# The pooled layer's input of one sequence moved out of its out-projection into the other sequence's pooled layer

## Chip, cores and metric

The kernel runs on one core of a Trainium2 chip. The metric is the device time of one execution in microseconds, as the median of several executions. TensorE is PE in all views (PEld its weight loads), VectorE is DVE, ScalarE ACT, GpSimd POOL, SyncE SP.

## What is computed

Two sequences of 1024 tokens and width 1024, the prompt (s = 0) and the sample (s = 1), go through two layers with shared weights. Layer 0 is attention with an out-projection, layer 1 a pooled layer. Cut to what matters here:

```python
def _pool_mixer(h, w_in, w_grp, scale, w_out):
    u, gate = jnp.split(h @ w_in, 2, axis=-1)
    pooled = win_sum / cnt - u32.reshape(b, s, POOL_GROUPS, POOL_GROUP_DIM)
    mixed = jnp.einsum('bsgc,gcd->bsgd', pooled.astype(h.dtype), w_grp)
    mixed = mixed * scale.reshape(POOL_GROUPS, POOL_GROUP_DIM)
    y = mixed.reshape(b, s, POOL_WIDTH) * jax.nn.silu(gate)
    return y @ w_out

for l in range(DEPTH):
    shift, scl, gate = jnp.split(mod[:, None, :], 3, axis=-1)
    h = _rmsnorm(x, pre_norm[l]) * (1.0 + scl) + shift
    m = _attn_mixer(h, ...) if l % 2 == 0 else _pool_mixer(h, ...)
    x = x + gate * _rmsnorm(m, post_norm[l])
```

All is float32. The kernel gets float32 products from pairs: each operand is split into a rounded part (hi) and the rest (lo), and three matmuls make one product. So every operand of a matmul needs a copy (hi) and a subtraction (lo).

## The kernel before

The order of the program is: layer 0 of the prompt (until about 816 us), its out-projection (`outproj0(0)`, to 943), the KV projection of the sample (to about 1003) and its attention, its out-projection (`outproj0(1)`, from about 1645 to 1760), the pooled layer of the sample (`layer1(1)`, to about 2052), the pooled layer of the prompt (`layer1(0)`). A scheduler orders the instructions of each engine from the program's order and its own costs; each engine then runs its list in order. Nearly all DMAs are issued by SP, in order. A DMA's completion goes to one of eight lanes, and a DMA waits for the one issued eight before it on its lane.

**Out-projection** (`outproj0`, L1039). Eight tiles of 128 tokens. For tile i PE makes y times w_out, 48 matmuls of 128x512 into a PSUM slot S of two (`out_mm`, L986 to L991); tiles 0 to 3 have their y split beforehand (yw), tiles 0 and 1 are mostly computed before the attention ends (`out_pre`). For tiles 4 to 7 y is loaded and split one tile ahead in `load_ys` (L1052; `load_y`, L978). Then, per tile: Square on ACT with the sum of squares (L1101), jk = S times pg on DVE (L1102), which frees the slot, the reciprocal root on POOL (L124, L126), xt = jk r + xt on DVE (L1104), and the DMA of xt to x1_d (L1105, in the views x_d). The xt and x1_d of a tile are of the form "(t m r) d -> t r m d": tile t holds 128 tokens in the permuted order that the attention uses. After that the input of the pooled layer is made: `normed` (L246: Square L249, for the prompt a product L252, for the sample product and addition L254, L255, on POOL except in the last two tiles) and, one tile later, eight transposes with `perm` (`turned`, L257, L263). For the prompt the result goes to DRAM (`put_stash`, L278: copies L284 and L282, DMA hs_d L285), for the sample to the split hT in SBUF (`put_hT`, L269). `run_h` takes a step of these transposes at every second k of a tile.

In `outproj0(0)` two other things run beside it: the first weights of the next stage (`prefetch`, eight ws of 128 KB, splits L329 and L330) and the layer-0 input of the sample: `h_affine` (L300) loads eight xk of 512 KB in tiles of the yh buffers and makes hT by hi (ACT, L319), product and sum (DVE, L320) and lo (L321, half on DVE, half on POOL).

**Pooled layer** (`layer1`, L1117). Four groups g of 256 channels. For each: u by two `lin` of 48 matmuls into S slots (three now), the windows on POOL and DVE (`pool_ct`), two gates (`lin` and `gate_ct`), the mixed product (`mixed`, L1202 ff.; yf L1206, y L1209, L1210), and after the u of group g the output product of group g - 1 (`outp`, 8 tiles of 12 matmuls, L1228 to L1230, added into m by DVE, L1252). The pooled layer of the prompt starts with `h_affine` from hs_d (L1126), before its first `lin` (`lin_c`, L1133 to L1135).

```python
            x_ = nc.tensor.transpose(T[:, k * P : (k + 1) * P], x[:, kk * P : (kk + 1) * P], idm)
...
            self.normed(op, xt[i], hx, jk, g1, sh1, nc.vector if i >= NT - 2 else None)
            put = self.put_stash(op, i, self.hs_d) if s == 0 else self.put_hT(hN, i)
            late = [self.turned(hx, perm, put)]
```

Of the kernel before, what the change touches and what calls it, by code (L numbers as in the profile page):

```python
# [13 lines left out]
P = 128  # L14
# [45 lines left out]
class Trunk:  # L60
# [196 lines left out]
    def turned(self, x, idm, put):  # L257
        nc = self.nc
        for b in range(2):
            T = self.ptile("T")  # L260
# [28 lines left out]
    def x_ahead(self, ap):  # L289
        nc = self.nc  # L290
        xv = self.t["xs"].rearrange("(hf p r) d -> r hf p d", hf=2, r=4)
        for i in range(NT):
            x = ap.tile([P, D], F32, name=self.n("xa"), tag="vb", bufs=2)
            nc.sync.dma_start(x, xv[i // 2, i % 2])
            yield
            xe = ap.tile([P, 2, 4, P], F32, name=self.n("xe"), tag="vb", bufs=2)
            self.normed(ap, x, x, xe.rearrange("p b k c -> p (b k c)"))
            yield
            yield from self.turned(x, self.ident, self.put_stash(ap, i, self.xn_d, one=xe))

    def h_affine(self, pool, hT, src, col, tags, bufs, ahead):
# [3 lines left out]
        def load():  # L305
            k = len(xk)
            if k < KT:
                xk.append(pool.tile([P, S], F32, name=self.n("xk"), tag=tags[k % len(tags)], bufs=bufs))
# [5 lines left out]
        for k in range(KT):  # L314
# [6 lines left out]
            (nc.gpsimd if k % 2 else nc.vector).tensor_tensor(lo, x, hi.bitcast(F32), ALU.subtract)  # L321
# [290 lines left out]
    def layer0(self, s, hT, ap, side, after_proj, open2, run_h, first=None):  # L612
# [67 lines left out]
        ahead = self.x_ahead(ap) if s == 0 else None  # L680
# [207 lines left out]
        def finish_A(h):  # L888
# [37 lines left out]
            nc.sync.dma_start(self.y_d[s, ch : ch + HD, :], z[HD:P])  # L926
# [112 lines left out]
    def outproj0(self, s, wo, op, hN, pre, prefetch):  # L1039
        nc, t = self.nc, self.t  # L1040
        xsrc = (t["xp"] if s == 0 else t["xs"]).rearrange("(t m r) d -> t r m d", m=32, r=4)
        x1o = self.x1_d[s].rearrange("(t m r) d -> t r m d", m=32, r=4)
        hq, late = [], []
        ys, xt = {}, {}
# [6 lines left out]
        def load_ys(i):  # L1051
            if 4 <= i < NT:  # L1052
                ys[i] = []
                for f in range(2):
                    y0 = op.tile([P, 4, P], F32, name=self.n("y0"), tag="y0", bufs=3 - s)
                    ys[i].append(op.tile([P, 2, 4, P], F32R, name=self.n("yh"), tag="yh", bufs=4))
                    self.load_y(s, i, y0, ys[i][f], 4 * f, 4 * f + 4, 0)
# [10 lines left out]
        perm = op.tile([P, P], F32, name=self.n("perm"), tag="perm")  # L1068
        pg = self.mrow(op, 0, s, 2, "pg")
        load(0)  # L1070
        load(1)
        nc.sync.dma_start(perm, t["k_perm"])
        hN_of = g1 = sh1 = None
# [6 lines left out]
        pf = prefetch(op)  # L1080
        for i in range(NT):
            if i >= 1:
                load(i + 2)
            if i >= 3:
                load_ys(i + 1)
            if i < 2:
                ps = pre[0][i]
            else:
                ps = self.ptile("S")
                for k in range(KT):  # L1090
                    yh, q = (pre[1][i], k) if i < 4 else (ys[i][k // 4], k % 4)
                    self.out_mm(ps, yh, q, wo, k, k == 0, k == KT - 1)
# [5 lines left out]
            hx = op.tile([P, D], F32, name=self.n("hx"), tag="hx", bufs=2)  # L1098
            ss = op.tile([P, 1], F32, name=self.n("ss"), tag="ss", bufs=6)
            jk = op.tile([P, D], F32, name=self.n("jk"), tag="jk", bufs=2)  # L1100
            nc.scalar.activation(hx, ps, AF.Square, accum_out=ss)  # L1101
            nc.vector.tensor_tensor(jk, ps, pg, ALU.mult)  # L1102
            r = self.rstd(op, ss, D, 1)
            nc.vector.scalar_tensor_tensor(xt[i], jk, r, xt[i], op0=ALU.mult, op1=ALU.add)  # L1104
# [7 lines left out]
        hq += late  # L1112
        for _ in pf:
            pass
        return run_h

    def layer1(self, s, hT, lp, hp, run_h, open_l2):  # L1117
# [4 lines left out]
        if s == 0:  # L1122
            hc = lp.tile([P, 2, KT], F32, name=self.n("hc"))
            nc.sync.dma_start(hc, self.mod_d[1, 0, 0:2].rearrange("c (k p) -> p c k", p=P))
            for _ in self.h_affine(lp, hT, self.hs_d, hc, ("sg1", "wa"), 2, 2):
                pass  # L1126
# [87 lines left out]
        def outp(parts, first, last, xs=None):  # L1214
            for i in range(NT):
                ps = self.ptile("S")
# [15 lines left out]
                if half:  # L1232
# [8 lines left out]
                    ss = lp.tile([P, 1], F32, name=self.n("ss"), tag="ss", bufs=4)  # L1241
# [11 lines left out]
                if last:  # L1253
                    ss = lp.tile([P, 1], F32, name=self.n("ss"), tag="ss", bufs=4)
# [21 lines left out]
        wu = wu0  # L1276
        for g in range(4):
            tail = s == 0 and g == 3
            wo = None
            if g and not tail:  # L1280
# [3 lines left out]
            for ct in range(2):  # L1284
                p = lp.tile([P, 2, S], F32R, name=self.n("pT"), tag="pT", bufs=2)
                pool_ct(g, pss[ct] if pss else lin(wu, ct), p)
                pT.append(p)
            if s == 1 and g == 0:
# [3 lines left out]
                self.psum("A", "SSS")  # L1292
            wgt = self.l1_block(wp, t["pwin"][2 * g + 1])
# [296 lines left out]
```

## Time and profile before

| what | value |
|---|---|
| median of 3 runs | 2353.71 us (2350.28 to 2356.88) |
| profiled execution, own time | 2351.0 us |
| its span, mean granted clock of TensorE | 2349.2 us, 0.964 |
| PE busy | 2140.3 us (91%) |
| DVE, ACT, POOL busy | 1562.4 (67%), 1065.3 (45%), 1009.8 us (43%) |
| DMA | 189.14 MB, 81 GB/s in the mean |

The busy shares are means over stages that differ. Where time could come from is read by stage: from the granted clock and the DMA share of a stretch, and from what PE waited for in it. The view of waits puts a wait down to the instruction or transfer that came last. A page's DMA digit is the busy share of the core's 16 DMA engines in tenths.

### The profile page before, as it was taken

Reading aid. Unit: us, or ns where it says so; the run is one execution under the profiler, and the core shown is the slowest. Engines: PE = TensorE matmul, PEld = TensorE weight load, DVE = VectorE, ACT = ScalarE, POOL = GpSimd, SP = SyncE. Lnnn points to the kernel's source line nnn. Section 1 sums busy time; section 2 is a strip of 40 time slices with the busy share of each in tenths; the row PEclk is TensorE's granted clock in tenths of the full one; section 3 lists DMA queues with packets and bytes.
Section 4 is the critical chain, followed back from the end, with each engine's and each line's share of the span. In section 5 each row is a group of like instructions: output and inputs, shape, how many; then the busy total and the mean of one; then the engine's idle time right before and its main releaser. Section 6 shows DMA issues by size and latency. Waiting matters only on the chain.

```text
span 2349.2 us, 38580 instructions
## 1 busy us (share of the span) xinstructions
PE 2140.3 (91%) x13777; PEld 1904.1 (81%) x13777; DVE 1562.4 (67%) x3463; ACT 1065.3 (45%) x2435; POOL 1009.8 (43%) x1445
## 2 busy tenths in 40 slices
PE   6998899999998776899999999987689999999998
PEld 3987788899998655898898999986468888778887
DVE  7788888776767653577778767776345455673536
ACT  6355555666666431256657666764221111320112
POOL 3776665123534332553321235343234345573552
PEclk9999999999999887999999999998899999999999
DMA  6123343111212353310011112122423111441113
GB/s 256 49 86 117 96 120 98 47 45 55 70 50 66 101 179 120 96 33 19 19 37 33 45 54 68 52 68 86 131 85 91 41 59 50 142 168 41 56 43 148
DMA packets 162641, 189.14 MB, mean 81 GB/s; under 512 B 16200, under 2 KB 127920, under 8 KB 162448
## 3 DMA queue, kind: packets, MB, share of 16 engines
q1 hardware_dynamic: 162112, 186.21, 25.3%
q8 instruction: 109, 1.79, 0.3%
q14 instruction: 84, 0.69, 0.1%
q10 hardware_dynamic: 144, 0.26, 0.0%
q0 software_dynamic: 192, 0.20, 0.0%
HBM read 144.43 MB, written 42.18 MB: 79 GB/s over the span
## 4 chain that ended last, share of the span: by engine, by line
PE 41%; DVE 7%; DMA 4%; ACT 3%; issue 2%; POOL 2%; SPq 1%; POOLq 0%; DVEq 0%; ACTq 0%
PE S L1135 5%; PE S L1134 5%; PE S L1133 5%; PE J L394 3%; PE J L396 3%; PE J L395 3%; PE S L1228 2%; PE S L1229 2%; PE S L1230 2%; PE H L720 2%; PE T L758 1%; DVE E L738 1%; DVE mx L721 1%; PE O L771 1%; DMA x_d<-xt 1%
## 5 line engine op out<-in xcount | busy, mean ns | idle before, releaser
L330 POOL TENSOR_TENSOR w<-ws,w 128x256 fp32r<-128x256 f32 (+1 forms) x418 | 391.9, 950 | 377.4 <-DVE w L329 266.0
L394 PE MATMUL J<-w,hT 128*128 128x256 f32 x1664 | 481.3, 289 | 2.9 <-ACT xj L407 2.1
L396 PE MATMUL J<-w,hT 128*128 128x256 f32 x1664 | 476.9, 287 | 3.1 <-DVE hT L1354 2.8
L395 PE MATMUL J<-w,hT 128*128 128x256 f32 x1664 | 477.5, 287 | 0.9 <-POOL w L330 0.7
L329 DVE CAST w<-ws 128x256 fp32r<-128x256 f32 (+1 forms) x420 | 186.9, 468 | 214.4 <-PE S L1135 77.9
L394 PEld LDWEIGHTS J<-w,hT 128*128 128x128 f32 x1664 | 318.0, 191 | 7.2 <-ACT xj L407 3.9
L396 PEld LDWEIGHTS J<-w,hT 128*128 128x128 f32 x1664 | 317.9, 191 | 5.6 <-DVE hT L1354 3.4
L395 PEld LDWEIGHTS J<-w,hT 128*128 128x128 f32 x1664 | 318.0, 191 | 4.3 <-POOL w L330 2.6
L738 DVE TENSOR_TENSOR E<-T,E 128x512 fp32r<-128x512 f32 x384 | 262.0, 684 | 83.3 <-ACT E L737 81.0
L737 ACT ACTIVATE E<-T 128x512 fp32r<-128x512 f32 x384 | 226.3, 597 | 200.0 <-PE T L758 72.5
L727 ACT ACTIVATE P<-H,mx 128x512 f32<-128x512 f32 x256 | 173.7, 685 | 109.4 <-DVE mx L722 95.5
L1135 PE MATMUL S<-hT,w 128*128 128x512 f32 x512 | 199.8, 391 | 2.7 <-POOL w L330 2.7
L1134 PE MATMUL S<-hT,w 128*128 128x512 f32 x512 | 200.0, 391 | 1.7 <-DVE hT L321 1.7
L1133 PE MATMUL S<-hT,w 128*128 128x512 f32 x512 | 199.3, 390 | 0.2 <-ACT hT L273 0.2
L721 DVE TENSOR_REDUCE mx<-H 128x1 f32<-128x512 f32 x256 | 173.7, 682 | 33.5 <-PE H L720 31.6
L758 PE MATMUL T<-identr,P 128*128 128x128 f32 x1024 | 163.1, 274 | 3.7 <-DVE E L738 3.1
L771 PE MATMUL O<-E,v 128*128 128x256 f32 x512 | 144.1, 303 | 16.1 <-DVE E L738 15.5
L837 ACT ACTIVATE P<-H,nm 128x256 f32<-128x256 f32 x256 | 117.7, 473 | 79.0 <-DVE nm L831 78.6
L770 PE MATMUL O<-E,v 128*128 128x256 f32 x512 | 147.5, 297 | 5.3 <-DVE X L792 2.8
L758 PEld LDWEIGHTS T<-identr,P 128*128 128x128 f32 x1024 | 123.0, 141 | 19.6 <-DVE E L738 2.4
L480 POOL TENSOR_TENSOR hl<-xj,hl 128x256 fp32r<-128x256 f32 x64 | 48.2, 756 | 208.7 <-DVE hl L479 154.6
L771 PEld LDWEIGHTS O<-E,v 128*128 128x128 f32 x512 | 97.2, 190 | 29.0 <-DVE E L738 26.7
(270 smaller groups left out, 5201.3 us busy)
## 6 DMA issues: line engine op xcount, KB each, us to landing
ws<-win SPq DMA_DIRECT2D x192, 128.0 KB
ws<-ada_w SPq DMA_DIRECT2D x128, 128.0 KB
ws<-pwin SPq DMA_DIRECT2D x60, 256.0 KB
vb<-v_d SPq DMA_DIRECT2D x64, 144.0 KB
xt<-xp SPq DMA_DIRECT2D x16, 512.0 KB
ada<-ada_w SPq DMA_DIRECT2D x16, 512.0 KB
y_d<-X SPq DMA_DIRECT2D x32, 256.0 KB
v_d<-v SPq DMA_DIRECT2D x64, 128.0 KB
```

The lines of the kernel that those rows point to most:

```text
L330: (nc.vector if dve_lo else nc.gpsimd).tensor_tensor(lo, src, hi.bitcast(F32), ALU.subtract)
L394: nc.tensor.matmul(ps, hi, w[:, 0, k, :], start=(k == 0), stop=False)
L395: nc.tensor.matmul(ps, hi, w[:, 1, k, :], start=False, stop=False)
L396: nc.tensor.matmul(ps, lo, w[:, 0, k, :], start=False, stop=(k == KT - 1))
L721: nc.vector.tensor_reduce(mx[:, c : c + 1], ps[c], axis=AX, op=ALU.max, negate=True)
L737: nc.scalar.activation(ov[0], Tv, AF.Copy)
L738: nc.vector.tensor_tensor(ov[1], Tv, ov[0].bitcast(F32), ALU.subtract)
L758: nc.tensor.transpose(T[:, (2 * e + i) * P : (2 * e + i + 1) * P], Pt[(h, 2 * g + i)][:, (2 * kp + e) * P : (2 * kp + e + 1) * P], self.ident)
L771: nc.tensor.matmul(O, st["v"][:, kk, :], pairs(ex, 1, e), start=False, stop=(kk == 7))
L1133: nc.tensor.matmul(ps[:, cs], w[:, 0, k, ws], hT[:, k, 0, cs], start=(k == 0), stop=False)
L1134: nc.tensor.matmul(ps[:, cs], w[:, 0, k, ws], hT[:, k, 1, cs], start=False, stop=False)
L1135: nc.tensor.matmul(ps[:, cs], w[:, 1, k, ws], hT[:, k, 0, cs], start=False, stop=(k == KT - 1))
```

## The change

- **The pooled layer's input of the prompt.** `outproj0(0)` ends a tile with the DMA to x1_d; second norm, transposes and hs_d are gone from it, and so is `perm`. `layer1(1)` has them instead: `x_ahead`, until now used in the attention, takes a source, a target and tags; for each of eight tiles it loads 128 rows of x1_d (plain order of tokens, one buffer xa), does `normed`, transposes into an S slot (`wide`) and writes hs_d. `more(n)` takes steps of it between u, outputs and gates of groups 0 to 3.
- **The affine step of the prompt** (`h_affine` from hs_d) moves from the start of `layer1(0)` into group 3 of `layer1(1)`: there the output product of group 2 comes behind the gates (`swap`), and each of its tiles is preceded by one step of `h_affine`. wo and the first weights of the next layer are loaded behind it.
- **Out-projections.** y of tile i + 2 is loaded at tile i (`load_y`) and split at k = 3 of the tile before (`split_y`); `prefetch` becomes `late_block` (four ws of 256 KB in the y0 buffers, from tile 6); xt has four buffers for the prompt; `h_affine` has two xk buffers of its own, starts at tile 1, and has its lo on POOL for odd k. For the sample the addition of `normed` is always on DVE. The order in which buffers are made differs.
- **The last y_d** of each attention is issued by ACT's queue.
- ss has six buffers in `layer1`.

```diff
-    def x_ahead(self, ap):
+    def x_ahead(self, ap, src, dst, tags, bufs, wide=False):
...
+            for _ in self.turned(x, self.ident, self.put_stash(ap, i, dst, one=xe), wide):
+                if not wide:
+                    yield
+            if wide:
+                yield
...
+    def late_block(self, wp, src):
+        nc = self.nc
+        self.wi += 1
+        w = (self.base if self.wi % 2 else wp).tile([P, 2, KT, 256], F32R, name=self.n("w"), tag="w", bufs=1)
+        ws = [wp.tile([P, 2, 256], F32, name=self.n("ws"), tag="y0", bufs=4) for _ in range(4)]
+        for q in range(4):
+            nc.sync.dma_start(ws[q], src[:, 2 * q : 2 * q + 2, :])
+        yield w
+        for q in range(4):
+            ks = slice(2 * q, 2 * q + 2)
+            self.split(w[:, 0, ks], w[:, 1, ks], ws[q])
             yield
...
-            nc.sync.dma_start(self.y_d[s, ch : ch + HD, :], z[HD:P])
+            (nc.scalar if h == heads[-1] else nc.sync).dma_start(self.y_d[s, ch : ch + HD, :], z[HD:P])
...
-                xt[i] = op.tile([P, D], F32, name=self.n("xt"), tag="xt", bufs=3)
+                xt[i] = op.tile([P, D], F32, name=self.n("xt"), tag="xt", bufs=4 - s)
...
+        def split_y(i):
+            if 4 <= i < NT:
+                if i > 4:
+                    new_y(i)
+                for y, z in zip(yh[i], y0[i]):
+                    nc.scalar.activation(y[:, 0], z, AF.Copy)
+                    nc.vector.tensor_tensor(y[:, 1], z, y[:, 0].bitcast(F32), ALU.subtract)
...
-            hN_of = self.h_affine(op, hN, self.xn_d, self.col[:, 1], ("yh",), 4, 3)
-            next(hN_of)
+            hN_of = self.h_affine(op, (("xk", 2),), 1, hN, self.xn_d, self.col[:, 1], (1, 3, 5, 7))
...
             if i >= 1:
                 load(i + 2)
-            if i >= 3:
-                load_ys(i + 1)
+            if i >= 2:
+                load_y(i + 2)
+            if i == 1 and hN_of:
+                next(hN_of)
...
-                        if i >= 4:
-                            next(pf, None)
+                    if k == 3:
+                        split_y(i + 1)
+                        if i == 6:
+                            pf = self.late_block(op, t["pwin"][0] if s else t["win"][8])
+                            self.kvw = next(pf)
...
-            self.normed(op, xt[i], hx, jk, g1, sh1, nc.vector if i >= NT - 2 else None)
-            put = self.put_stash(op, i, self.hs_d) if s == 0 else self.put_hT(hN, i)
-            late = [self.turned(hx, perm, put)]
-            if hN_of:
+            if s:
+                self.normed(op, xt[i], hx, jk[i], g1, sh1, nc.vector)
+                late = [self.turned(hx, perm, self.put_hT(hN, i))]
+            if hN_of and i >= 2:
...
+        if s == 1:
+            ahead = self.x_ahead(lp, lambda i: self.x1_d[0, i * P : (i + 1) * P, :], self.hs_d, ("xa", "yf"), 1, True)
...
+            if swap:
+                more(99)
+                hc = lp.tile([P, 2, KT], F32, name=self.n("hc"))
+                nc.sync.dma_start(hc, self.mod_d[1, 0, 0:2].rearrange("c (k p) -> p c k", p=P))
+                hNext = Halves(self, hp)
+                h_of = self.h_affine(lp, (("wa", 2), ("u", 2), ("wa", 2), ("u", 2), ("xa", 1)), 2, hNext, self.hs_d, hc, (1, 3, 5, 7))
+                next(h_of)
+                outp(prev, False, False, each=lambda i: next(h_of))
+                prev = []
```

**What moves on the engines.** Lines after the change have its own numbers; x_d is x1_d, y the buffers y0.

SP at the start of the prompt's out-projection. Before:

```order
L926 DMA y_d<-X_10884 64x1024
L243 DMA row_10922<-mod_d 128x1024
L1049 DMA xt_10924<-xp 128x1x1024
L1049 DMA xt_10926<-xp 128x1x1024
L1072 DMA perm_10921<-k_perm 128x128
L309 DMA xk_10929<-xn_d 128x1024
L309 DMA xk_10931<-xn_d 128x1024
L309 DMA xk_10933<-xn_d 128x1024
L1049 DMA xt_10935<-xp 128x1x1024
L309 DMA xk_10955<-xn_d 128x1024
L981 DMA y_1798_11090<-y_d 128x4x128
L981 DMA y_1800_11095<-y_d 128x4x128
```

With the change:

```order
L243 DMA row_10921<-mod_d 128x1024
L1072 DMA xt_10924<-xp 128x1x1024
L1072 DMA xt_10926<-xp 128x1x1024
L1072 DMA xt_10928<-xp 128x1x1024
L1072 DMA xt_10941<-xp 128x1x1024
L317 DMA xk_10943<-xn_d 128x1024
L1081 DMA y_1770_10957<-y_d 128x4x128
L1081 DMA y_1771_10958<-y_d 128x4x128
L317 DMA xk_11020<-xn_d 128x1024
L1081 DMA y_1780_11032<-y_d 128x4x128
L1081 DMA y_1781_11033<-y_d 128x4x128
L1147 DMA x_d<-xt_10924 4x32x1024
```

The last y_d has left SP's list, so row and the first xt stand behind loads of y alone. All four first xt come ahead of the first xk, and the loads of y for tiles 4 and 5 ahead of the first x_d; no hs_d stands between them.

DVE in the prompt's out-projection, about tile 4. Each jk frees a PSUM slot; xk and col belong to `h_affine`, ws and w to the weights of the next stage. Before:

```order
L983 TENSOR_TENSOR yh_11192<-y_1816_11191,yh_11192 128x512
L1102 TENSOR_TENSOR jk_11167<-S_11100,row_10922 128x1024
L320 TENSOR_SCALAR xk_11080<-xk_11080,col 128x1024
L1104 SCALAR_TENSOR_TENSOR xt_10965<-jk_11167,rr_11172,xt_10965 128x1024
L329 CAST w_11222<-ws_11247 128x256
L282 COPY hl_11244<-T_11239 128x512
L983 TENSOR_TENSOR yh_11197<-y_1818_11196,yh_11197 128x512
L983 TENSOR_TENSOR yh_11304<-y_1839_11303,yh_11304 128x512
L252 TENSOR_SCALAR hx_11165<-xt_10965,rr_11180 128x1024
L329 CAST w_11222<-ws_11263 128x256
L1102 TENSOR_TENSOR jk_11285<-S_11201,row_10922 128x1024
```

With the change:

```order
L328 TENSOR_SCALAR xk_11099<-xk_11099,col 128x1024
L1144 TENSOR_TENSOR jk_11089<-S_11036,row_10921 128x1024
L328 TENSOR_SCALAR xk_11104<-xk_11104,col 128x1024
L329 TENSOR_TENSOR hT_10917<-xk_11104,hT_10917 128x1024
L1146 SCALAR_TENSOR_TENSOR xt_10941<-jk_11089,rr_11095,xt_10941 128x1024
L1089 TENSOR_TENSOR yh_11221<-y_1790_11111,yh_11221 128x512
L328 TENSOR_SCALAR xk_11180<-xk_11180,col 128x1024
L328 TENSOR_SCALAR xk_11185<-xk_11185,col 128x1024
L329 TENSOR_TENSOR hT_10917<-xk_11185,hT_10917 128x1024
L350 CAST w_11300<-ws_11301 128x512
L1144 TENSOR_TENSOR jk_11170<-S_11115,row_10921 128x1024
```

The products of the second norm (L252) and the copies hl are gone. jk of tile 3 (jk_11089) stands behind the product of the fourth xk, and jk of tile 4 (jk_11170) behind the products of xk five to seven and the cast of the first ws. Seven rows later, with the casts of the other three ws ahead of it, follows the jk of tile 5.

DVE at the boundary of the pooled layers: m collects the output products, xk and hT belong to the affine step of the prompt. Before, with the last y of the sample and the last output product:

```order
L1210 TENSOR_TENSOR y_3580_23135<-yf_23133,y_3580_23135 128x1024
L1206 SCALAR_TENSOR_TENSOR yf_23151<-S_23138,sccol,sg_23100 128x1024
L320 TENSOR_SCALAR xk_23364<-xk_23364,hc_23362 128x1024
L321 TENSOR_TENSOR hT_23360<-xk_23364,hT_23360 128x1024
L320 TENSOR_SCALAR xk_23383<-xk_23383,hc_23362 128x1024
L1210 TENSOR_TENSOR y_3583_23153<-yf_23151,y_3583_23153 128x1024
L320 TENSOR_SCALAR xk_23393<-xk_23393,hc_23362 128x1024
L329 CAST w_23103<-ws_23116 128x512
L1252 TENSOR_TENSOR m_21615<-S_23156,m_21615 128x1024
```

With the change, the output product of group 2:

```order
L328 TENSOR_SCALAR xk_22936<-xk_22936,hc_22932 128x1024
L329 TENSOR_TENSOR hT_22934<-xk_22936,hT_22934 128x1024
L328 TENSOR_SCALAR xk_22938<-xk_22938,hc_22932 128x1024
L350 CAST w_23088<-ws_23089 128x512
L350 CAST w_23088<-ws_23093 128x512
L350 CAST w_23088<-ws_23097 128x512
L328 TENSOR_SCALAR xk_22959<-xk_22959,hc_22932 128x1024
L328 TENSOR_SCALAR xk_22940<-xk_22940,hc_22932 128x1024
L1291 TENSOR_TENSOR m_21389<-S_22945,m_21389 128x1024
L1228 SCALAR_TENSOR_TENSOR sg_22929<-sg_22929,S_22880 128x1024
L329 TENSOR_TENSOR hT_22934<-xk_22940,hT_22934 128x1024
```

The products of xk now stand among the additions of the output product of group 2, a gate and a mixed product earlier than before; the first of these additions (S_22945) is behind four of them and three casts.

## Rows read from the trace of the kernel before

**Rows 1.** The page, part 2: granted clock and DMA share in 40 slices.

```profile
PEclk9999999999999887999999999998899999999999
DMA  6123343111212353310011112122423111441113
```

**Rows 2.** Stages: length, busy time (instructions) by engine, clock, DMA share, GB/s.

```profile
821.80:943.00 121.20, 85.68 (x339) 68.02 (x339) 48.39 (x55) 32.44 (x50) 33.29 (x40) 0.85 0.49 150
943.00:1002.70 59.70, 53.09 (x441) 52.09 (x440) 34.33 (x79) 18.29 (x49) 31.98 (x50) 0.97 0.28 87
1651.20:1760.40 109.20, 84.95 (x337) 67.16 (x338) 45.94 (x49) 25.09 (x46) 30.70 (x40) 0.85 0.32 106
1760.40:2024.10 263.70, 263.45 (x1168) 217.51 (x1166) 130.17 (x135) 37.92 (x40) 115.43 (x95) 1.00 0.19 62
2024.10:2075.00 50.90, 41.62 (x168) 33.44 (x169) 48.29 (x36) 18.12 (x24) 41.31 (x29) 0.93 0.58 210
```

**Rows 3.** PE's waits, 816 to 1005 us: us in total, times, longest.

```profile
PE T L263 <- DVE hx L252: 21.4, 5, 6.9
PE S L989 <- ACT yh L982: 7.6, 1, 7.6
PE S L989 <- DVE jk L1102: 5.3, 2, 2.8
PE T L415 <- DVE hl L552: 3.9, 2, 3.5
PE T L263 <- DMA perm<-k_perm: 3.7, 1, 3.7
```

**Rows 4.** PE's waits, 1640 to 1765 us.

```profile
PE T L263 <- POOL hx L255: 22.2, 5, 8.4
PE S L989 <- DVE jk L1102: 8.3, 2, 6.2
```

**Rows 5.** PE's waits, 2015 to 2075 us.

```profile
PE S L1135 <- POOL w L330: 2.7, 1, 2.7
PE S L1134 <- DVE hT L321: 1.7, 1, 1.7
```

**Rows 6.** DMA share, GB/s in slices: 860 to 900; GB/s: 2020 to 2060.

```profile
DMA  3893922232222752225784559622773472562212
GB/s 112 195 364 139 303 102 102 111 102 102 111 98 102 234 172 102 111 102 181 249 249 128 137 154 286 210 99 102 249 200 114 150 258 102 187 210 78 78 57 95
...
GB/s 8 123 270 127 4 0 0 0 53 221 397 418 410 410 371 211 393 406 363 326 412 389 191 37 170 92 0 0 0 0 193 332 0 0 172 352 86 279 373 397
```

**Rows 7.** DMA issues, 816 to 945 us; SP's longest wait, 1640 to 1765.

```profile
hs_d<-hl SPq DMA_DIRECT2D x12, 256.0 KB
...
SPq L1049 <- DMA x_d<-xt: 29.1, 5, 9.5
```

**Rows 8.** PE's timeline (start, length); a chain row, 1690 to 1760 us.

```profile
1760.43 0.40 PE L1134 MATMUL S<-hT,w 128*128 128x512 f32 x1
...
1764.97 0.39 PE L1133 MATMUL S<-hT,w 128*128 128x512 f32 x1
...
1751.77 0.44 PE T L263 x4
```

**Rows 9.** PE's timeline, 940 to 980; a chain row, 816 to 1005 us.

```profile
955.19 0.66 PE L263 MATMUL T<-perm,hx 128*128 128x128 f32 x4 [2.46 <-DVE hx L252]
...
953.40 10.31 DMA hs_d<-hl
```

**Rows 10.** DVE's timeline, 1645 to 1672 us.

```profile
1649.94 1.23 DVE L1102 TENSOR_TENSOR jk<-S,row 128x1024 f32<-128x1024 f32 x1 [8.88 <-DMA row<-mod_d]
...
1664.22 1.28 DVE L254 SCALAR_TENSOR_TENSOR hx<-xt,rr,row 128x1024 f32<-128x1024 f32 x1 [5.89 <-DMA row<-mod_d]
```

**Rows 11.** Groups by line, shape, 1650 to 1760 us: busy, mean ns, idle.

```profile
L255 POOL TENSOR_TENSOR hx<-hx,row 128x1024 f32<-128x1024 f32 x6 | 14.5, 2420 | 12.4 <-DVE hx L254 6.2 <-DMA row<-mod_d 4.6 <-DMA y<-y_d 1.6
```

**Rows 12.** Groups by line, 2028 to 2075 us.

```profile
L320 DVE TENSOR_SCALAR xk<-xk,hc 128x1024 f32<-128x1024 f32 x6 | 8.8, 1473 | 1.1 <-ACT hT L319 1.1
```

More of the change, by code (lines that the diff above doesn't have):

```diff
@@ L307, in load @@
             if k < KT:
-                xk.append(pool.tile([P, S], F32, name=self.n("xk"), tag=tags[k % len(tags)], bufs=bufs))
+                tag, bufs = tags[k % len(tags)]
+                xk.append(pool.tile([P, S], F32, name=self.n("xk"), tag=tag, bufs=bufs))
                 nc.sync.dma_start(xk[k], src[k])
@@ L679, in layer0 @@
         rest = self.ada_rest(ap) if s == 0 else None
-        ahead = self.x_ahead(ap) if s == 0 else None
+        xv = self.t["xs"].rearrange("(hf p r) d -> r hf p d", hf=2, r=4)
+        ahead = s == 0 and self.x_ahead(ap, lambda i: xv[i // 2, i % 2], self.xn_d, ("vb", "vb"), 2)
         started = {0, 1, 2}
@@ L1121, in layer1 @@
         wu0 = kvw or self.l1_block(wp, t["pwin"][0])
[L1122 to L1126, printed above, removed]
         outap = t["yp"] if s == 0 else t["ys"]
@@ L1212, in mixed, with outp @@
             return yT
-        def outp(parts, first, last, xs=None):
+        def outp(parts, first, last, xs=None, each=None):
             for i in range(NT):
+                if each:
+                    each(i)
                 ps = self.ptile("S")
@@ L1253, in outp @@
                 if last:
-                    ss = lp.tile([P, 1], F32, name=self.n("ss"), tag="ss", bufs=4)
+                    ss = lp.tile([P, 1], F32, name=self.n("ss"), tag="ss", bufs=6)
                     if xs:
@@ L1276, in layer1, with more @@
         wu = wu0
+        ahead = hNext = h_of = None
+        if s == 1:
+            ahead = self.x_ahead(lp, lambda i: self.x1_d[0, i * P : (i + 1) * P, :], self.hs_d, ("xa", "yf"), 1, True)
+        def more(n):
+            for _ in range(n):
+                if ahead:
+                    next(ahead, None)
         for g in range(4):
             tail = s == 0 and g == 3
+            swap = s == 1 and g == 3
             wo = None
-            if g and not tail:
+            if g and not tail and not swap:
                 prev[0] = (prev[0][0], self.l1_block(wp, t["pwout"][g - 1]))
@@ L1287, in layer1 @@
                 pT.append(p)
+                if g:
+                    more(1)
             if s == 1 and g == 0:
@@ L1292, in layer1 @@
                 self.psum("A", "SSS")
+                more(2)
             wgt = self.l1_block(wp, t["pwin"][2 * g + 1])
@@ L1297, in layer1 @@
             self.split(wg[:, 0], wg[:, 1], ws)
-            if g and not tail:
-                outp(prev, g == 1, False)
+            if g and not tail and not swap:
+                outp(prev, g == 1, False, each=lambda i: more(i % 2))
                 prev = []
-            elif tail:
+            elif tail or swap:
                 prev[0] = (prev[0][0], self.l1_block(wp, t["pwout"][2]))
@@ L1304, in layer1 @@
                 wu = self.l1_block(wp, t["pwin"][2 * g + 2])
-            elif s == 1:
+            sgs = []
+            for ct in range(2):
+                sgs.append(gate_ct(lin(wgt, ct)))
+                more(1 if g else 2)
+            if swap:
[7 more added lines that the diff above has]
+                prev = []
+            if g == 3:
                 wo = self.l1_block(wp, t["pwout"][3])
-            sgs = [gate_ct(lin(wgt, ct)) for ct in range(2)]
-            if g == 3:
                 if s == 1:
                     self.kvw = self.l1_block(wp, t["pwin"][0])
-                else:
-                    wo = self.l1_block(wp, t["pwout"][3])
             ys = xs = None
@@ L1441, in run @@
             c_op, op = self.pool("op", R)
-            def prefetch(sp):
-                self.wi = 0
-                out = []
-                yield from self.block_gen(None, sp, t["pwin"][0] if s else t["win"][8], out=out, bufs=1 + s)
-                self.kvw = out[0]
-            run_h = self.outproj0(s, after.wo, op, hT, pre, prefetch)
+            run_h = self.outproj0(s, after.wo, op, hT, pre)
             st["c"].__exit__(None, None, None)
```

72 lines of the change are left out of this document (41 added, 31 removed).

## The prediction

> **What bounds the kernel now.** Start with the slices of the page: PE is nearly full except in two dips, around slices 14 to 16 and 28 to 29, and there the granted clock falls and the DMA digits rise to 5 and 4 [rows 1]. The table by stage gives these dips a name [rows 2]: the out-projection of the prompt (821.8 to 943.0, PE 85.7 busy of 121.2 us at clock 0.85) and that of the sample (1651.2 to 1760.4, 85.0 of 109.2, also 0.85). Between the second dip and 2024.1 PE has 263.5 of 263.7 us at clock 1.00: there every instruction added to PE adds its whole length. The list of PE's waits in each dip says what ends the idle time: in the first, the transposes T wait for hx (21.4 us, 2.5 of it behind the stretch) and for perm (3.7), the matmuls S for yh (7.6) and jk (5.3) [rows 3]; in the second, T waits for hx, made on POOL (22.2), and S for jk (8.3) [rows 4]. At the boundary of the two pooled layers PE waits 2.7 and 1.7 us in the first matmuls of the prompt's [rows 5].
>
> That is what the engines show. What stands behind hx and yh is the DMA digits. While xt is loaded or x_d written, they sit at 2 tenths for many slices together, with about 102 GB/s; in the pooled layer, where other transfers run, about 410 GB/s are reached [rows 6]. So a 512 KB xt or x_d takes 524 KB / 102 GB/s = 5.1 us on about a fifth of the engines, and another 512 KB transfer (xk, xa) 1.3 us on all. Each out-projection has eight xt and eight x_d. In the sample's, SP waited 29.1 us for earlier x_d before it could send the next xt, which is the same queue seen from the other end [rows 7].
>
> The Trainium skill has the reason (DMA: Bandwidth & Descriptors, "Why a DMA increments its semaphore by 16 and not by 1"): a transfer is spread over the largest number of engines up to 16 that divides the outermost dimensions of both sides, and takes the lowest-numbered ones. The write x_d has 4 there, and the trace agrees with its 2 tenths of 16 engines. It speaks against the change: these transfers keep their shape, so by it an out-projection can't come down to PE's own time; without it the sum below would be that of the first rival.
>
> **A. Out-projection of the prompt.** Removed: 48 of the 64 transposes and their waits, Square, product and copies of the second norm, and 12 of the 16 hs_d writes [rows 7]. The four xt buffers, y two tiles ahead and the split before its tile take away the waits for hx, perm and yh, (21.4 - 2.5) + 3.7 + 7.6 = 30.2 us. PE's own need: twenty matmuls go by in 1764.97 - 1760.43 = 4.54 us [rows 8], so a tile of 48 takes 10.9 us, six 65 us, and with the first jk wait and a few matmuls at the lower clock about 71 of 121. That would save 50. But tile 7 needs its slot, so jk of tile 5; this stands in DVE's order behind the cast of the fourth ws, which stands on SP behind x_d of tile 4. Before it come xt1 to xt7 and x_d0 to x_d4, 12 x 5.1 = 61 us; xk, 8 x 1.3 = 10; y and ws, 12 x 0.65 = 8. From 821.8 (xt1 waits for the last matmul of tile 1) that is 901 with no gap. I add 5 for issues that come late, since SP waits in order for DVE's xt and for earlier landings: 906; then 2 for cast and jk, 1 for yh, 12.5 for tile 7 (part at the low clock): 921.5 against 943.0. **A = -21.** Bounds: -50 (PE alone) and 0 (summed in this way, with 12 hs_d of 0.65 [rows 7], the old stretch has 8 us of transfers more and comes to 107 at most, and it took 121: if its other gaps come back, little is won). I take the value of the transfers, since the rows they come from are of this very stage.
>
> What is late next: jk3 stands behind the affine step of xk3, and this behind x_d0, x_d1, xt4 and xt5 in the DMA queues; so tiles 5, 6 and 7 should each wait for jk. Its own ACT queue for the last y_d wins nothing at the start: row comes earlier, xt1 doesn't.
>
> **B. KV projection (59.7 us).** The last transposes leave it, 16 at 0.44 us per four [rows 8], 1.8, with a wait of 2.5 for hx and the 3.9 for hl [rows 3, 9]; the latter came from DVE, held by an hs_d write of 10.3 [rows 9]. Together 8.2; late next are raw and ropB, which SP sends behind x_d of tile 6. **B = -5**, between 0 and -8.
>
> **C. Out-projection of the sample.** Nothing changes before about 1666: jk1 stands behind hx0, which needs the second row, landed at 1664.2 [rows 10]. The addition on DVE costs 1.2, like jk of the same size [rows 10], instead of 2.4 on POOL, six times [rows 11], on an engine busy 45.9 of 109.2 [rows 2]; POOL's 14.5 us go. From tile 3 PE alone needs 5 x 10.9 + 10 x 0.44 = 59, so the end would be 1726 (-34). By transfers: the third row and xt2 stand behind the second row, so they end about 1664.2 + 1.3 + 5.1 = 1671; then come 2 y, x_d0, x_d1, xt3 to xt6, x_d2 to x_d4, the other y and ws: 9 x 5.1 + 8 x 0.65 = 51, so 1722 to 1724; late issues 4, jk 2, tile 7 with four transposes 12: 1742. **C = -18**, between -34 and -6 (only the 8.4 of one wait for hx goes).
>
> **D. Pooled layer of the sample.** Added to PE: 64 transposes, 16 x 0.44 = +7.0, in a stage that has no idle time. Loads of 1.3 us and steps on DVE, ACT and POOL lie beside it: they are busy 130, 38 and 115 of 264 us [rows 2]. Removed at the boundary: 2.7 + 1.7 [rows 5], as hT of the prompt is made an output stage and a mixed stage earlier; the granted clock of 0.93 over those 51 us [rows 2] may give 1 back with the waits gone. New: the adds of output stage 2 now stand on DVE among the affine steps of xk, 8 x 1.5 [rows 12] and 4 x 1.2, and the first xk can't be read before the last hs_d is written. The stage has 8 tiles of 12 matmuls, 21.8 us by [rows 8], with 8 adds of the size of jk, 1.23 [rows 10]; so DVE has 26.6 us for 21.8, and I let PE wait for some of the excess, 3. +7.0 - 4.4 - 1 + 3 = **D = +4**, between -3 and +15.
>
> **Sum.** -21 - 5 - 18 + 4 = -40. The profiled execution took 2351.0 us (span 2349.2), the median of the runs 2353.7, which is 2.7 more; -40 from the median gives **2314 us**. A difference under 0.3%, 7 us, can't be told from none here.
>
> **Rivals.** *PE alone sets the out-projections*: the engines that xt leaves free take the rest, y and xk are never late, and A = -50, B = -8, C = -34, D = +4: 2266. For it: the waits of PE name DVE, ACT and POOL, not DMA [rows 3, 4]. Against: the flat 2 tenths [rows 6]. Something between the two, -45 to -75, is as likely as the full case.
>
> *Old gaps in new places*: DVE's strict order lets each late xk or ws hold jk, A = -8, C = -8, B = -3, D = +6: -13, 2341. For it: the old stretch took 14 us more than its transfers and last tile add up to.
>
> *Slower*: x_ahead has one xa and one xe buffer. Its transposes stand in PE's queue between the matmuls of the projections, so if a tile isn't ready, PE stops. A tile goes through the load, Square, rstd, the product, copies and the write of the one before; an hs_d write took 10.3 us beside other transfers [rows 9]. Each tile has more steps ahead of it than one lin of 10.9 us; but where loads of weights stand ahead, the wait could be 6 us for each of 8 tiles, +48, and with A + B + C = -44 the sum is +4 + 4: 2362. It decides from 5 us a tile on. For it: nowhere is PE as full as there, so there is nothing to hide it. Against: DMA is used at 0.19 there [rows 2], and transfers move at 400 GB/s.
>
> *It doesn't do what it says*: DVE and POOL set the slots of the output stage as before and the lower clock of each new gap takes the rest: within 7 us of before.
>
> **How the numbers follow.** The forecast (savings of 25 to 55) has 0.58, PE alone or half way to it 0.20, old gaps in new places 0.13, slower 0.06, no change 0.03. So faster 0.91, same 0.03, slower 0.06. The range for 8 in 10: its low end, 2272, is between the first rival half way (-65: 2289) and in full (2266), its high end, 2342, just above the second; what lies below and above holds about 0.08 and 0.10.
>
> **What would show it.** Right: waits T for hx gone from the prompt's out-projection, DMA digits at 2 tenths through most of it, waits of S for jk in front of tiles 5, 6 and 7, tile 7 ending 95 to 105 us after tile 1; about 91 us from tile 2 to 7 in the sample's; the pooled layer of the sample 5 to 10 us longer in PE, with no wait of transposes for xa over 1 us. Wrong: the out-projections at clock 1.00 without gaps (first rival), or single waits of 5 us on the S slots of the transposes (slower).

## The result and the profile after

The change made the kernel slower: 2369.65 us in the median (2367.53 to 2371.39) against 2352.89 (2350.28 to 2356.88) in the same session, a ratio of 1.0069 with a 95% interval of 1.0052 to 1.0087. The forecast was 40 us less; the result is 17 us more, outside the range.

The two profiled spans differ by 20.4 us (2369.6 and 2349.2). Cut at the same points of the program in PE's timeline, the difference lies here (us; the last two columns are runs of the section on the experiments):

| stage | before | after | after, split xt | before, split xt |
|---|---|---|---|---|
| start to the end of tile 1 of the prompt | 821.8 | 824.5 | 821.8 | 819.9 |
| prompt's out-projection, to the end of tile 7 | 121.2 | 115.4 | 73.9 | 75.5 |
| KV projection, to the first score matmul | 59.7 | 53.1 | 52.6 | 54.2 |
| attention, to the end of tile 1 of the sample | 642.3 | 643.0 | 643.2 | 644.6 |
| sample's out-projection, to the end of tile 7 | 115.4 | 122.6 | 80.9 | 79.9 |
| pooled layer of the sample | 292.1 | 318.5 | 309.3 | 293.1 |
| pooled layer of the prompt | 296.7 | 292.5 | 292.9 | 296.5 |

The prompt's out-projection won 6, the KV projection 7, the last layer 4; the sample's out-projection lost 7 and the sample's pooled layer 26. The time to the end of tile 1 lay between 819.7 and 824.5 us in all profiled runs of this study, so its 2.7 us are put down to no part of the change.

On the page the dips of the clock are slices 13 to 16 and 27 to 30, where before they were 14 to 16 and, counted in the same way, 29 and 30 [rows 1]. A slice is 59 us long, so 13 and 27 lie ahead of the out-projections; what the stages lost is read from the rows by stage below.

```profile
PEclk9999999999998878999999999988889999999999
DMA  6124333111212343200011121133323223341113
```

The stages, in the columns of [rows 2]:

```profile
824.50:939.90 115.40, 76.87 (x289) 61.15 (x290) 39.80 (x38) 20.45 (x30) 24.01 (x22) 0.81 0.42 125
939.90:993.00 53.10, 50.70 (x426) 49.45 (x425) 31.87 (x76) 16.21 (x45) 30.92 (x48) 1.00 0.24 81
1636.00:1758.60 122.60, 80.73 (x337) 64.25 (x338) 48.77 (x52) 25.38 (x48) 18.57 (x32) 0.83 0.33 103
1758.60:2077.10 318.50, 304.71 (x1330) 247.31 (x1329) 168.42 (x177) 67.13 (x84) 143.33 (x126) 0.97 0.32 97
```

The out-projections have a lower clock than before (0.81 and 0.83 after 0.85 and 0.85), and the pooled layer of the sample is no longer at 1.00. PE's waits in the first of them, where [rows 3] had four kinds (the fifth, for hl, stands behind the stage):

```profile
PE S L1011 <- DVE jk L1144: 38.6, 5, 15.1
```

One kind is left, but it is longer than all the old ones of that stage together: the 18.9 us for hx (21.4 without the 2.5 behind the stage), 3.7 for perm and 7.6 for yh went, jk grew from 5.3 to 38.6. In the sample's, against [rows 4]:

```profile
PE S L1011 <- DVE jk L1144: 24.1, 2, 19.0
PE T L267 <- DVE hx L255: 17.7, 3, 9.9
```

And in the pooled layer of the sample, where before there was no wait over 0.3 us until its end:

```profile
PE S L267 <- ACT xe L288: 6.7, 2, 5.5
PE S L1267 <- DVE m L1291: 2.7, 2, 2.5
PE S L1269 <- DVE y L1247: 1.9, 1, 1.9
PE S L267 <- DVE xa L252: 1.2, 1, 1.2
```

The last stage no longer has the waits of [rows 5], as forecast.

### The profile page after: what moved, and what is told of

It reads as the page before. It is cut to its first block, busy times and chain, and to the rows that moved or that the text cites. A ratio compares the mean times of both kernels' runs of the same rounds, so it can differ in the third digit from the quotient of the medians.

```text
span 2369.6 us, 38555 instructions
## 1 busy us (share of the span) xinstructions
PE 2147.6 (91%) x13777; PEld 1905.4 (80%) x13777; DVE 1558.7 (66%) x3461; ACT 1065.1 (45%) x2435; POOL 991.7 (42%) x1431
```

## The experiments

**Theory 1**: both out-projections are set by the xt loads and x1_d writes, which occupy few DMA engines; casts and affine steps in front of jk pass the lateness on to PE. The pooled layer lost by the transposes, their waits and the clock behind them. **Theory 2**: the order of DVE and SP costs the time whatever the transfers' shape, and the moved affine step costs the pooled layer.

**Split transfers, in the changed kernel and in the one before.** The same edit in both:

```diff
-                nc.sync.dma_start(xt[i], xsrc[i])
+                for q in range(4):
+                    nc.sync.dma_start(xt[i][32 * q : 32 * q + 32], xsrc[i][q])
...
-            nc.sync.dma_start(x1o[i], xt[i])
+            for q in range(4):
+                nc.sync.dma_start(x1o[i][q], xt[i][32 * q : 32 * q + 32])
```

> The changed kernel with every xt load and x1_d write of the out-projections as four DMAs of 32 rows instead of one of 4 x 32 rows. Theory 1 (these transfers, on about a fifth of the DMA engines, set both out-projections, by way of the casts and affine steps that stand before jk on DVE): the flat 2 tenths vanish, the prompt's out-projection falls from 115 us (824.5 to 939.9) to 75 to 85, the sample's from 123 (1636.0 to 1758.6) to 85 to 95, the run to 2295 to 2310. Theory 2 (DVE's order and SP's in-order waits cost the time whatever the transfers' shape; four times the issues make it worse): 2360 to 2385.

> The kernel before with the same split of the xt and x1_d transfers. Theory 1: its out-projections lose the part of the waits for hx, yh and jk that came from late transfers, 121 to 85-100 and 115 to 85-100 us, the run 2295 to 2320. Theory 2: the waits for hx made on DVE and POOL stay, 2345 to 2360.

Measured: 2284.66 us for the changed kernel (2276.39 to 2287.2), ratio to before 0.9708 (0.9682 to 0.9734); 2270.26 for the one before (2265.6 to 2270.32), ratio 0.9653 (0.9632 to 0.9674). One edit at two places took 85 and 82 us. The waits that Theory 2 expected to stay went (for hx PE waits 0.4 us in the prompt's out-projection of the second, where it had been 18.9), so Theory 1 holds; both runs came out below its ranges, by 10 and 25 us, so it was too modest. The DMA share and GB/s in slices, first 860 to 900 us of the changed kernel, then 825 to 865 of it with the split, both inside the prompt's out-projection:

```profile
DMA  4739222288489722222222211057947998322222
GB/s 142 233 127 234 86 98 111 102 185 308 139 153 284 188 82 98 98 115 98 102 111 102 111 74 45 12 74 205 266 102 143 303 190 197 88 98 98 111 102 102
```

```profile
DMA  9999689889756999989999999899999949888769
GB/s 250 254 258 352 205 238 168 238 361 340 275 180 171 338 278 356 279 279 264 227 187 289 291 332 347 164 344 406 353 334 280 217 98 225 266 111 319 143 213 381
```

The flat 2 tenths at 98 to 115 GB/s are gone. The stages (columns as above; prompt's and sample's out-projection, pooled layer of the sample), first of the changed kernel with the split, then of the one before with it:

```profile
821.80:895.70 73.90, 67.86 (x290) 55.43 (x291) 40.63 (x38) 20.75 (x30) 23.70 (x22) 0.98 0.71 199
1591.50:1672.40 80.90, 74.96 (x337) 60.80 (x338) 48.64 (x52) 25.70 (x48) 18.21 (x32) 0.96 0.58 157
1672.40:1981.70 309.30, 299.48 (x1330) 244.04 (x1329) 169.70 (x177) 67.31 (x84) 143.60 (x126) 0.99 0.33 100
```

```profile
819.90:895.40 75.50, 72.33 (x339) 58.97 (x339) 50.98 (x55) 32.56 (x50) 30.40 (x40) 1.00 0.81 239
1594.20:1674.10 79.90, 74.15 (x337) 60.22 (x338) 49.71 (x50) 25.62 (x48) 33.47 (x42) 0.96 0.56 159
1674.10:1967.20 293.10, 288.04 (x1266) 237.54 (x1265) 156.61 (x156) 52.03 (x58) 135.77 (x109) 0.99 0.23 75
```

Two things follow. The old out-projection of the prompt, with its 48 transposes and the second norm, takes 75.5 us once its transfers are fast, the new one without them 73.9: on this footing the work that the change moved out costs 1.6 us there, and most of the 50 that the forecast's bound had put down to it was the transfers'. And on this footing the change still loses 14 us, since the pooled layer of the sample takes 309.3 instead of 293.1.

**Half of the split** (only the second hunk above, in the changed kernel):

> The changed kernel with the x1_d writes alone as four DMAs; the xt loads stay one DMA each. If the busy time of those few DMA engines is what counts, half of it goes: out-projections of 80 to 92 us (prompt) and 88 to 100 (sample), the run 2300 to 2325. If it is SP's in-order wait for the completion of an x1_d write (26.8 us in the prompt's) that counts, nearly all of the split's gain comes back: 2284 to 2295.

Measured: 2330.19 us (2326.01 to 2331.35), ratio 0.9900 (0.9881 to 0.9920). The two out-projections:

```profile
823.40:922.30 98.90, 74.22 (x290) 59.32 (x291) 40.25 (x38) 20.49 (x30) 25.47 (x22) 0.88 0.52 149
1618.60:1725.60 107.00, 83.63 (x337) 66.72 (x338) 49.18 (x52) 25.52 (x48) 18.43 (x32) 0.87 0.41 119
```

98.9 lies between 115.4 and 73.9 and 107.0 between 122.6 and 80.9, at about 40%; the run got 39 of the 85 us. It came out 5 us over the expected range, and each out-projection 7 us over its own, but far from the other case: half of the slow bytes, nearly half of the gain. This does not part the two cases cleanly, because SP's waits of an xt for an x_d did not go with the edit. SP's waits, the prompt's and then the sample's:

```profile
SPq L1072 <- DMA x_d<-xt: 13.3, 4, 7.9
SPq L1072 <- DMA x_d<-xt: 15.7, 6, 7.7
```

In the changed kernel they were 26.8 and 41.2 us, and with both kinds of transfer split there is none in the prompt's and 8.0 in the sample's. Of what they lose in all, the wait had lost 13 of 27 us in the prompt's and the time 17 of 41; in the sample's the wait had lost 25 of 33 us and the time only 16 of 42. So in the sample's at least, SP's wait alone does not account for the time, and the engines' busy time counts.

**The casts off DVE.** In late_block:

```diff
-            self.split(w[:, 0, ks], w[:, 1, ks], ws[q])
+            nc.gpsimd.tensor_copy(w[:, 0, ks], ws[q])
+            nc.gpsimd.tensor_tensor(w[:, 1, ks], ws[q], w[:, 0, ks].bitcast(F32), ALU.subtract)
```

> The changed kernel with both halves of the split of the late weights (late_block) on POOL, so that no cast of a late ws stands before jk on DVE; the transfers stay as they are. If the casts' place in DVE's order passes the late transfers on to PE: the wait of 19.0 us in the sample's out-projection goes and some of the prompt's, 123 to 100-110 and 115 to 105-112 us, the run 2345 to 2358. If late xt hold jk by way of their own step just as long: 2365 to 2372.

Measured: 2360.63 us (2355.28 to 2363.85), ratio to before 1.0037 (1.0025 to 1.0049), so 9 us under the changed kernel and between the two cases. The out-projections took 106.0 and 117.2 us, the second over the 110 that the first case allowed. PE's waits in the sample's, then DVE's wait behind them and POOL's behind that:

```profile
PE T L267 <- DVE hx L255: 32.5, 3, 24.1
PE S L1012 <- DVE jk L1145: 5.4, 1, 5.4
```

```profile
DVE xt L1147 <- POOL rr L126: 32.1, 2, 29.0
POOL w L342 <- DMA ws<-pwin: 38.8, 3, 31.6
```

The wait of 19.0 for jk is gone, and a longer one for hx has come: now POOL stands at a cast with ws late, the reciprocal root rr behind it, DVE's xt behind that. The place of the casts decides which engine is caught, and moves some microseconds; the lateness itself is the transfers'.

**No transposes in the pooled layer of the sample** (the copies read the untransposed rows, so the prompt's output lacks the transposition):

```diff
             if wide:
-                T2 = T2 if b else self.ptile("S")
-                T = T2[:, 512 * b : 512 * b + 512]
...
+                put(b, x[:, 512 * b : 512 * b + 512].rearrange("p (k c) -> p k c", k=4))
+                yield
+                continue
```

> The changed kernel without the 64 transposes of the prompt's rows in the sample's pooled layer: the copies take the untransposed rows, so the prompt's output lacks the transposition. If the transposes, their waits for copies (6.7 and 1.2 us) and the lower clock after these waits cost the pooled layer its time: 15 to 20 less, 2349 to 2355. If the moved affine step does: only their own 7 to 9 us, 2361 to 2363.

Measured: 2343.66 us (2341.63 to 2347.07), ratio to before 0.9966 (0.9956 to 0.9975): 26 us less than the changed kernel, more than expected of the transposes, and by itself enough to turn the result round. The pooled layer of the sample:

```profile
1753.10:2048.30 295.20, 290.18 (x1266) 236.24 (x1265) 172.97 (x177) 67.70 (x84) 147.32 (x126) 0.99 0.34 105
```

That is 3.1 over the 292.1 of before: the loads, norms and copies of x_ahead and the affine step inside output stage 2 lie almost wholly beside PE's work, though DVE has 173 us to do there instead of 156.

**The affine step back at the start of the last layer** (`swap = False`, and `h_affine` before the first `lin` as in the kernel before):

> The changed kernel with the output product of group 2 before the gates and the affine step of the prompt at the start of its own pooled layer, as in the kernel before. If the transposes are what costs: the waits of 2.5 and 1.9 us go, those of the boundary (4.8, 2.7, 1.7) come back, 2365 to 2375. If the affine step inside output stage 2 costs: 2350 to 2360.

Measured: 2370.69 us (2369.82 to 2372.85), ratio 1.0081 (1.0062 to 1.0100), as against 1.0069. This is the case in which the transposes cost the time: the pooled layer of the sample keeps 317.8 us. In this profile the last layer is back at 296.6 us after 292.5, but the run is only 1.0 us longer, inside the noise, so no gain or loss of the run is shown for this part of the change.

**Copies behind all eight transposes.** The second four had waited for ACT's copy of the first four, 5.5 us once:

```diff
+        if wide:
+            T2 = self.ptile("S")
+            for kk in range(8):
+                nc.tensor.transpose(T2[:, kk * P : (kk + 1) * P], x[:, kk * P : (kk + 1) * P], idm)
+            for b in range(2):
+                put(b, T2[:, 512 * b : 512 * b + 512].rearrange("p (k c) -> p k c", k=4))
+            yield
+            return
```

> The changed kernel with all eight transposes of a tile of x_ahead ahead of its two copies, so that the second four no longer wait for ACT's copy of the first four. If these waits and the lower clock behind them are what the transposes cost beyond their own 7 us: the waits for xe (6.7) and some 4 of clock go, the pooled layer of the sample falls from 318.5 to 305 to 310, the run to 2356 to 2362. If 64 transposes cost a full PE the same wherever they stand: 2366 to 2372.

> The same order in the kernel with the split xt transfers (2284.7). If the waits for xe count: 2272 to 2280, still no better than the kernel before with the split (2270.3), since the transposes' own 7 us stay. If not: 2282 to 2287.

Measured: 2367.81 us (2365.2 to 2368.66), ratio 1.0065 (1.0049 to 1.0080), not to be told from the changed kernel; with the split transfers 2275.77 (2273.24 to 2279.37), ratio 0.9676 (0.9660 to 0.9693) after 0.9708. That is in the range expected if the waits for xe count, but the two intervals overlap. Without the split the first case missed: the wait moved. PE's waits in the pooled layer of the sample, without the split:

```profile
PE S L262 <- DVE xa L252: 6.5, 1, 6.5
PE S L1275 <- DVE m L1299: 3.1, 2, 2.5
PE S L1277 <- DVE y L1255: 1.9, 1, 1.9
PE S L1178 <- DVE xe L294: 1.5, 1, 1.5
```

The 6.7 for ACT's copy of xe are gone, and the transposes now wait 6.5 for the product that makes xa.

**Transposes of a resident tile** (the same kernel, the transposes read the identity instead of xa, so the prompt's output lacks its rows):

```diff
-                nc.tensor.transpose(T2[:, kk * P : (kk + 1) * P], x[:, kk * P : (kk + 1) * P], idm)
+                nc.tensor.transpose(T2[:, kk * P : (kk + 1) * P], idm, idm)
```

> The kernel of the run before with copies last (2367.8), with the 64 transposes reading the resident identity in place of the rows of the tile, so that they never wait for load, norm or product; the prompt's output lacks its rows. If waits for the rows and the lower clock behind them make up what the transposes cost beyond their own 7 us: the wait of 6.5 goes and some 4 of clock, 2354 to 2358, the pooled layer of the sample 302 to 307 after 314. If the slots of PSUM that they hold or their place in PE's list cost it: 2362 to 2368.

Measured: 2357.83 us (2351.61 to 2361.03), ratio 1.0026 (1.0015 to 1.0037), in the range of the first case; the pooled layer of the sample took 308.2 us, 1 more than that case allowed. The wait for xa is gone; the two longest of the others:

```profile
PE S L1275 <- DVE m L1299: 2.9, 2, 2.4
PE S L1178 <- DVE sg L1236: 2.7, 1, 2.7
```

Beside the run without transposes (295.2 us) the 64 ready ones cost 13.0. PE's waits there add up to 9.4, in the run without to 5.0, so 4.4 are waits for slots and for what DVE and ACT do about them, and 8.6 are left for the transposes, at a mean clock of 0.99 in both: 0.54 us for four where I had put 0.44. With copies last and rows to wait for, the stage took 314.1, 5.9 more; with the copies between, 318.5, another 4.4. Each of these lengths is from one profile. By the ratios of the runs to the kernel before, the same three steps are 14, 9 and 1 us, and the last is inside the noise: that the order of the copies costs anything is not shown.

**The step of x_ahead later, and the two best kernels side by side.** With split transfers and copies last:

```diff
-                more(1 if g else 2)
+                more(1)
```

> The kernel with the split transfers and copies last (2275.8), with one step of x_ahead in place of two behind each gate of group 0, so that load, norm and transposes of the second tile are a lin apart. If its wait for xa (3.2) and the clock behind it go: 2268 to 2273, level with the kernel before with the split (2270.3). If the later steps only move the wait to group 3, where the affine step needs the last tile: 2274 to 2282.

> The kernel before with the split transfers once more, on the same chip as the run above for a direct comparison: 2265 to 2272. If the moved work pays once the transfers are fast, the run above lies under it by over 3; if not, level or over it.

Measured: 2274.37 us (2272.93 to 2277.65), ratio 0.9680 (0.9666 to 0.9693), and 2266.61 (2262.59 to 2269.2), ratio 0.9643 (0.9628 to 0.9658). The first time is in the range of the second case. The waits for xa are gone, and one wait for y stands at the end of the stage, where the kernel before with the split has 4.8 (whether the later steps of x_ahead cause it was not traced):

```profile
PE S L1277 <- ACT y L1256: 8.0, 1, 8.0
```

So in direct comparison the kernel before with the split is 8 us faster than the best form of the change that I tried. Their ranges don't overlap. It beats both kernels of this study, the one before by 3.6% (3.4 to 3.7).

## Why the prediction was wrong

**A, the prompt's out-projection: -21 said, -6 measured.** The chain was right: jk of tile 3 stood behind the affine step of the fourth xk, jk of tile 4 behind the first cast, jk of tile 5 behind the fourth; tiles 5, 6 and 7 waited 15.1, 8.8 and 6.8 us for them, and the waits for hx, perm and yh were gone. A wait of 6.3 us in front of tile 4 had not been forecast. What was mis-sized is "12 x 5.1 = 61 us ... 901 with no gap. I add 5": the fourth cast ran at 924.5, 100 us after the end of tile 1, where 906, 84 us after it, was forecast. DVE's timeline, then SP's waits in this stage (us in total, times, longest):

```profile
924.53 0.43 DVE L350 CAST w<-ws 128x512 fp32r<-128x512 f32 x1 [3.14 <-DMA ws<-win]
924.87 1.22 DVE L1144 TENSOR_TENSOR jk<-S,row 128x1024 f32<-128x1024 f32 x1
```

```profile
SPq L1072 <- DMA x_d<-xt: 26.8, 3, 13.9
SPq L338 <- DVE yh L1089: 13.5, 1, 13.5
```

The bandwidth of one slow transfer was read correctly, but the sum treated the queue as nearly always full. SP sends in order and waits: an xt is not sent before the x_d that frees its buffer has completed, and the fourth ws not before DVE has split the y whose buffer it takes, behind the last xk and two more casts. In the slices of 860 to 900 us shown above, the digits fall to 1 and 0 at 883 to 885, ahead of an xt that SP sends at 884.8 after such a wait. The 5 us put for this were too few; how much of the 16 us each wait makes was not worked out. The bound of 0 that I had put to A came nearer the truth, and for the reason that stands there: the old stretch had not kept to its sum either, by 14 us.

**B: -5 said, -7 measured.** Right; raw and ropB, for which some 3 us had been kept, left no wait of PE in this stage, and 2 us of waits for hl stayed.

**C, the sample's out-projection: -18 said, +7 measured.** The step that failed is "after 1671 come ... 51, so 1722 to 1724; late issues 4". DVE's timeline at the worst point, [idle before <- releaser] in brackets:

```profile
1718.94 0.43 DVE L350 CAST w<-ws 128x512 fp32r<-128x512 f32 x1 [26.98 <-DMA ws<-pwin]
1719.29 1.22 DVE L1144 TENSOR_TENSOR jk<-S,row 128x1024 f32<-128x1024 f32 x1
...
1734.26 0.43 DVE L350 CAST w<-ws 128x512 fp32r<-128x512 f32 x1 [4.60 <-DMA ws<-pwin]
1734.61 1.22 DVE L255 TENSOR_TENSOR hx<-hx,row 128x1024 f32<-128x1024 f32 x1
```

DVE stands 27 us at the cast of the first ws; jk behind it, and PE 19.0 for jk. PE's 9.9 for hx end behind the cast of the fourth, which ran 98 us into the stage; the forecast's 1726 to 1728 are 81 to 83 us into it. The first ws was late because it was sent late. SP's timeline, start and length of each entry:

```profile
1680.36 0.55 SPq L1147 DMA_DIRECT2D x_d<-xt  x1
1696.42 0.54 SPq L1072 DMA_DIRECT2D xt<-xs  x1
1697.06 0.55 SPq L1147 DMA_DIRECT2D x_d<-xt  x1
1710.26 0.54 SPq L1072 DMA_DIRECT2D xt<-xs  x1
1710.89 0.43 SPq L338 DMA_DIRECT2D ws<-pwin  x1
```

After the x_d at 1680.4 SP sends nothing for 15.5 us: the next xt waits for that x_d to complete, 13 us pass before the xt after it, for the same reason, and only then comes the first ws, which lands 8 us later. The reason is that the sample's xt still has three buffers, where the prompt's now has four: each xt takes the buffer of the x_d three tiles before it. SP's waits of an xt for an x_d add up to 41.2 us in this stage, after 29.1 before [rows 7]. The change made it worse than before: it put four larger ws behind xt of tile 6 in SP's list, and their casts in front of jk in DVE's. In the kernel before, SP had sent the first ws at 1661.8, ahead of the first x_d. I had noticed both orders and counted only the bytes between them. My lower bound, -6, left out that a stage can grow.

**D, the pooled layers: +4 said, +22 measured** (26 in the sample's, -4 in the prompt's). The failing step is "+7.0 - 4.4 - 1 + 3": it gave the transposes their bare length and the waits 3 us. The -4.4 came: the last layer is 4.2 us shorter. Without the transposes the run was 26 us shorter, and the sample's pooled layer 23.3: 8.6 for their own time, 4.4 for waits for slots and what hangs on them, 5.9 for waits for rows, and 4.4 between the two orders of the copies, a part that the runs do not bear out. The rival that I gave 0.06, transposes waiting in a full PE, is thus nearest to what decided the sign, and its mark, a single wait of 5 us on a slot of the transposes, came with 5.5 us. The transposes cost some 3 us a tile in the mean where that rival had 6 of waiting, and this was enough because the wins that had to pay for it were not 44 but 5. Behind some of these waits the clock also fell, to a mean of 0.97 over this stage after 0.99. PE's timeline behind the longest wait of the stage (start, length), of the changed kernel:

```profile
1806.58 1.11 PE L267 MATMUL S<-identr,xa 128*128 128x128 f32 x4 [5.47 <-ACT xe L288]
...
1808.77 0.63 PE L1170 MATMUL S<-hT,w 128*128 128x512 f32 x1
1809.20 0.63 PE L1171 MATMUL S<-hT,w 128*128 128x512 f32 x1
...
1812.53 0.40 PE L1170 MATMUL S<-hT,w 128*128 128x512 f32 x1
1812.77 0.40 PE L1171 MATMUL S<-hT,w 128*128 128x512 f32 x1
```

The matmuls start 0.43 us apart at first, which is the lower of the clock's two levels, and 0.24 from 1812.5 on.

**The sum.** -21 - 5 - 18 + 4 = -40 was forecast; the table has -5.8 - 6.6 + 7.2 + 26.4 - 4.2 = +17.0, with 3.4 of start and attention the 20.4 between the two profiled spans.

**The engines of these transfers.** That xt and x_d sat at 2 tenths of the 16 engines, and no longer did once they were split, is in the slices above. "Why a DMA increments its semaphore by 16 and not by 1" in the Trainium skill (DMA: Bandwidth & Descriptors) gives four engines for transfers of this shape; the trace agrees with it. In "Rules for kernel authors" the same page of the Trainium skill advises one transfer in place of two over halves of the partitions, because both halves run on all 16 engines anyway. Its reason did not hold here, where the whole ran on few engines, and the measurement decides: 85 and 82 us less with four parts. I had used the rule of the engines to bound the gain and not turned it round: the same row of digits that capped the change named the edit that was worth 82 us.

That waits for x_d and not some other traffic hold SP in C is read from the trace; a kernel in which only the order of SP's list differs, or the sample's xt has a fourth buffer, was not run. Nor was the sample's jk, to which the change leaves one buffer in place of two (`bufs=2 - s`), tried alone; with split transfers the sample's out-projection takes 80.9 us in the changed kernel and 79.9 in the one before, so what else differs between them costs little there. The 2 to 3 us of the start and the attention were not looked into.

## What to carry to other kernels

When DMA digits sit flat at a low value for many slices, look at the shape of the transfers in them before costing anything else: here PE's list of waits named DVE, ACT and POOL, and the gain came from two kinds of DMA. Sum transfers only where the queue is kept full; where an in-order issuer waits for completions, count the waits. Work moved into a stage that has no idle time on PE costs its own length and each wait that it brings, and a stage that looks full of waits may give little back when the work leaves.

## What the runs showed of the hardware

Each load of xt and write of x1_d as four DMAs of 32 rows, in place of one of 4 x 32 rows, took the out-projections of the changed kernel from 115.4 and 122.6 us to 73.9 and 80.9, at 199 and 157 GB/s in the mean of the stage instead of 125 and 103. The best kernel has these four times as many issues on SP; what they cost by themselves was not measured. Transposes of 128x128, four in a row, cost a full stage 0.54 us, by the difference of two profiles, where a row of the chain had shown 0.44 [rows 8].
